# Two PSUM banks for the convolutions, ordered transfers in the even mixer, splits ahead of a norm and a shorter end in a two-layer decoder trunk

## The chip, the cores and the metric

The kernel runs on one core of a Trainium2 chip. The metric is the device time of one execution in microseconds (us), from which span, waits and clock are told apart by a profile of one such execution. Engines are called as in the profile: PE is TensorE (its matrix products), PEld its weight loads, DVE is VectorE, ACT ScalarE, POOL GpSimd; SP is a queue that only issues transfers. PE's clock has two levels, 1.2 and 2.4 GHz; a granted clock of 1.00 is the upper one, 0.50 the lower.

## What is computed

A trunk of two layers for 256 prompt tokens and 8 sample tokens of the same weights, model width 1024, inner width 2816 of each feed-forward network (FFN):

```python
def run_trunk(x, ...):
    for layer in range(DEPTH):                    # DEPTH = 2
        x = x + 0.5 * swiglu(rmsnorm(x, norm_g[layer, 0]), ff_in[layer, 0], ff_out[layer, 0])
        hn = rmsnorm(x, norm_g[layer, 1])
        # layer 0: even_mixer, layer 1: odd_mixer
        x = x + mix
        x = x + 0.5 * swiglu(rmsnorm(x, norm_g[layer, 2]), ff_in[layer, 1], ff_out[layer, 1])
    return rmsnorm(x, norm_f)

def even_mixer(h, s0, ...):      # gated linear attention beside a chunked spatial gate
    q, k, v, r, z, u_sg, v_sg = jnp.split(h @ w_in, EVEN_SPLITS, axis=-1)
    o, s_new = gla_recurrence(q, k, v, log_a, s0)
    out_a = rmsnorm(o, gla_g) * jax.nn.silu(r)
    out_b = gelu(u_sg) * (w_s @ layernorm(gelu(v_sg)) + sg_b)
    return jnp.concatenate([out_a, out_b], axis=-1) @ w_out, s_new, ...

def odd_mixer(h, conv_buf, pool_buf, ...):   # causal depthwise convolution beside causal pooling
    a, gt, xp = jnp.split(h @ w_in, ODD_SPLITS, axis=-1)
    out_c = jax.nn.silu(layernorm(depthwise_conv31(a * sigmoid(gt)) + conv_b))
    out_d = (mean of the last 2, 4, 8, 16 rows of xp, less xp) @ pool_w * pool_scale
    return jnp.concatenate([out_c, out_d], axis=-1) @ w_out, ...
```

The states of attention (gla), gate (sgv), convolution and pooling are outputs too.

## The kernel before, in words

Activations lie transposed, channels on the 128 partitions and T = 264 columns (256 prompt, 8 sample) in the free dimension. Every projection is a row of products 128 x 128 by 128 x 264. The weights are streamed: SP's queue loads chunks `raw` of 512 KB, ACT rounds each 128 x 1024 half of one to `hi`, DVE forms the rest `lo = raw - hi` (the "splits"), and PE makes three products for each block: activation's high part by `hi`, its low part by `hi`, its high part by `lo`. Tiles named `..h` and `..l` (`xh`, `xl`, `oyh`, `oyl`, `oah`, `oal`) are such high and low parts of activations.

The program is one instruction stream for each engine, written by Python code that runs generators (one for each task, such as `conv(i)`, `pooled(i)`, `sample_state(p)`) against a `Clock`: a planner that assigns each instruction a cost and a due time, and emits a split (`split_ahead`) when the engine is thought to be free. A task waits by `need` for what others `produce`, and by `acquire` for a buffer; `slot()` waits for a place between products. On the chip each engine runs its stream in this order, whatever is ready. Transfers that do not pass `keep_in_program_order` may be placed elsewhere in their queue by the scheduler behind the program.

Stages, in order: start, `ff00` (FFN of layer 0, first), even mixer (projections `evin_c`, output `ev_o`), `ff01`, `ff10`, odd mixer (`odin_c`, output `od_o`), `ff11` (the last FFN), end. A norm is a sum of squares (`odn_acc`, split in `ff_nh`, `ff_nl`, summed over partitions by PE to `ff_ss`) and a reciprocal root on DVE (`ff_v` to `ff_rb`) of nine steps; the projection runs before the norm is known, and `rb` is multiplied in when a column leaves PSUM. While `cur["chain"]` is set, between the last `od_o` column and the end of that root, `split_ahead` holds back lo splits that are more than one half chunk ahead of use.

In an FFN, column pairs a and g leave PSUM as `ff_ta = a * rb`, `ff_sa = silu(ff_ta)` (ACT) and `ff_g = g * ff_sa`; `g`'s `rb` is applied at the residual, `ff11n_r = ff_o * rb * 0.5`, `x += ff11n_r`.

In the even mixer the sample states S (2 of 512 KB) are loaded on POOL's queue, then `vb`, copies of the sample values spread over partitions (4 of 256 KB); ACT copies the layer-normed gate rows as `gv`, `vln`, which PE transposes (`trvln`).

In the odd mixer, ACT writes 32 copies `rr` of the gated values (8 for each of four channel groups), POOL's queue shifts each into place by a transfer, and `conv(i)` is 128 quarter products into a PSUM tile of the one `s2` buffer of 1024 columns, which ACT empties into `cv_i`. Their mean `mu` is a product again; DVE subtracts it. The pools are sums of shifted rows on DVE (`pw`, `pd`), one product `pp` each, which ACT and DVE split to `oyh`, `oyl`.

At the end ACT squares the last residual, PE sums (`fin_ss`), DVE takes a root of three columns (`rsqrt`, `fin_yi` and on), PE spreads it (`fin_pb`) and DVE multiplies; products `warm` of no use keep PE going in between.

## Time and profile before

| | |
|---|---|
| runs | 990.77, 988.93, 988.32 us; median 988.93 us |
| profiled execution | 990.54 us, of it the span of the trace 988.8 us |
| mean granted clock | 0.993 |
| busy share | PE 98%, PEld 96%, DVE 68%, ACT 50%, POOL 5% |
| chain that ended last | PE 91%, DVE 4%, ACT 2%, DMA 1%, issue 1% |
| transfers | 176.22 MB, mean 178 GB/s |

A busy PE means that a product is under way, not that it runs at full rate, since products overlap and the clock can be halved. So two views matter beside busy time: what each engine waited for, and the granted clock by stretches. In a timeline a row begins with start and length in us, and the bracket at its end is the engine's idle time ahead of it and what ended that. In a row of stretches come the length and then, for PE, PEld, DVE, ACT and POOL in turn, busy us and number of instructions.

### The profile page before, as it was taken

How to read it: one execution, taken by the hardware profiler on the slowest of the kernel's cores; microseconds unless marked ns; L12 is line 12 of the kernel's file. 1: busy time of each engine (PE TensorE's matmuls, PEld its weight loads, DVE VectorE, ACT ScalarE, POOL GpSimd, SP SyncE). 2: the span in 40 equal slices, each digit the busy share in tenths (PEclk: the TensorE clock that was granted, in tenths of full speed). 3: DMA queues.
4: the chain of work that ended last, by engine and by line, in shares of the span. 5: the costliest groups of instructions: out<-in, count | busy, mean ns of one | idle time of the engine just before them, and what ended most of it. 6: DMA issues, size and time to landing. Idle time of an engine off the chain costs nothing.

```text
span 988.8 us, 20086 instructions
## 1 busy us (share of the span) xinstructions
PE 970.9 (98%) x8258; PEld 953.7 (96%) x8258; DVE 671.3 (68%) x1072; ACT 493.1 (50%) x749; POOL 45.4 (5%) x105
## 2 busy tenths in 40 slices
PE   8999999999999999999999999999989999999997
PEld 7999999999899999999999999999978999999996
DVE  7866656678898876665667666566756886666552
ACT  6644444456376454444445444444474744444440
POOL 2000000030100000000000000000070000000000
PEclk9999999999999999999999999999999999999999
DMA  8755555562646575555555555555452566555531
GB/s 280 232 197 189 175 186 177 176 219 91 163 146 221 187 220 188 177 189 183 181 170 194 190 175 189 182 180 187 158 163 87 171 223 202 176 188 182 181 107 44
DMA packets 50555, 176.22 MB, mean 178 GB/s; under 512 B 6352, under 2 KB 6816, under 8 KB 50464
## 3 DMA queue, kind: packets, MB, share of 16 engines
q1 hardware_dynamic: 46800, 165.85, 51.0%
q0 software_dynamic: 3376, 8.68, 3.2%
q8 instruction: 65, 1.06, 0.5%
q10 hardware_dynamic: 288, 0.41, 0.1%
q14 instruction: 26, 0.21, 0.1%
HBM read 170.33 MB, written 3.42 MB: 176 GB/s over the span
## 4 chain that ended last, share of the span: by engine, by line
PE 91%; DVE 4%; ACT 2%; DMA 1%; issue 1%; SPq 0%; DVEq 0%; ACTq 0%
PE ff_c L316 50%; PE ff_o L316 26%; PE evin_c L316 5%; PE ev_o L316 2%; PE od_o L316 2%; PE odin_c L316 2%; DMA raw<-in_wts 1%; ACT rr L339 1%; PE conv L324 1%; DVE lo L339 1%; DVE start_xl L339 0%; DVE pd L339 0%; PE fin_ss L316 0%; PE o L316 0%; PE os L316 0%
## 5 line engine op out<-in xcount | busy, mean ns | idle before, releaser
L339 ACT ACTIVATE hi<-raw 128x1024 fp32r<-128x1024 f32 (+1 forms) x315 | 330.1, 1050 | 379.6 <-PE ff_c L316 207.9
L339 DVE TENSOR_TENSOR lo<-raw,hi 128x1024 fp32r<-128x1024 f32 (+1 forms) x315 | 382.0, 1216 | 162.0 <-ACT hi L339 160.9
L316 PE MATMUL ff_o<-ff_gh,hi 128*128 128x264 f32 x704 | 198.9, 283 | 0.0
L316 PE MATMUL ff_o<-ff_gl,hi 128*128 128x264 f32 x704 | 198.8, 282 | 0.0
L316 PE MATMUL ff_o<-ff_gh,lo 128*128 128x264 f32 x704 | 198.8, 282 | 0.0
L316 PEld LDWEIGHTS ff_o<-ff_gh,hi 128*128 128x128 f32 x704 | 132.1, 188 | 0.0
L316 PEld LDWEIGHTS ff_o<-ff_gh,lo 128*128 128x128 f32 x704 | 132.2, 188 | 0.0
L316 PEld LDWEIGHTS ff_o<-ff_gl,hi 128*128 128x128 f32 x704 | 132.2, 188 | 0.0
L316 PE MATMUL ff_c<-odn_xh,lo 128*128 128x264 f32 x352 | 99.8, 284 | 1.8 <-DVE lo L339 1.8
L316 PE MATMUL ff_c<-start_xh,lo 128*128 128x264 f32 x352 | 100.2, 285 | 1.1 <-DVE lo L339 1.1
L316 PE MATMUL ff_c<-start_xh,hi 128*128 128x264 f32 x352 | 99.9, 284 | 0.8 <-ACT hi L339 0.8
L316 PE MATMUL ff_c<-start_xl,hi 128*128 128x264 f32 x352 | 100.1, 284 | 0.0
L316 PE MATMUL ff_c<-odn_xh,hi 128*128 128x264 f32 x352 | 99.7, 283 | 0.0
L316 PE MATMUL ff_c<-odn_xl,hi 128*128 128x264 f32 x352 | 99.7, 283 | 0.0
L316 PE MATMUL ff_c<-ff01n_xh,lo 128*128 128x264 f32 x352 | 99.4, 283 | 0.0
L316 PE MATMUL ff_c<-ff01n_xh,hi 128*128 128x264 f32 x352 | 99.4, 282 | 0.0
L316 PE MATMUL ff_c<-ff01n_xl,hi 128*128 128x264 f32 x352 | 99.4, 282 | 0.0
L316 PE MATMUL ff_c<-evn_xl,hi 128*128 128x264 f32 x352 | 99.4, 282 | 0.0
L316 PE MATMUL ff_c<-evn_xh,hi 128*128 128x264 f32 x352 | 99.4, 282 | 0.0
L316 PE MATMUL ff_c<-evn_xh,lo 128*128 128x264 f32 x352 | 99.4, 282 | 0.0
L339 DVE TENSOR_TENSOR ff_g<-ff_c,ff_sa 128x264 f32<-128x264 f32 x88 | 37.7, 431 | 55.5 <-PE ff_c L316 55.5
L316 PEld LDWEIGHTS ff_c<-odn_xh,lo 128*128 128x128 f32 x352 | 66.6, 189 | 2.0 <-DVE lo L339 2.0
(366 smaller groups left out, 1927.7 us busy)
## 6 DMA issues: line engine op xcount, KB each, us to landing
raw<-in_wts SPq DMA_DIRECT2D x308, 512.0 KB, 3.4
raw<-in_wts SPq DMA_DIRECT2D x8, 256.0 KB, 5.1
rr<-gp POOLq DMA_DIRECT2D x32, 35.5 KB, 3.6
x<-in_xt SPq DMA_DIRECT2D x4, 264.0 KB, 4.7
S<-in_sgla POOLq DMA_DIRECT2D x2, 512.0 KB, 6.9
vb<-vbd POOLq DMA_DIRECT2D x4, 256.0 KB, 10.5
out_gla_s<-S POOLq DMA_DIRECT2D x2, 512.0 KB, 4.8
mat<-in_mats POOLq DMA_DIRECT2D x1, 640.0 KB, 5.2
```

Of the source, the lines that this page charges most:

```text
L316: return pe_run(nc.tensor.matmul(out, lhsT=lhsT, rhs=rhs, start=start, stop=stop), out, lhsT, rhs, cost)
L324: Clock.credit -= pe_run(nc.tensor.matmul(out, lhsT=lhsT, rhs=rhs, start=start, stop=stop), out, lhsT, rhs, cost)
L339: ins = tc.keep_in_program_order(f(*args, **kw))
```

## The change

Eight edits: the four convolutions share one PSUM tile and take its two banks (512 columns) in turn, and the planner's credit is not left negative behind them; the pools' products no longer wait for a slot; the root of three columns has seven steps in place of nine; in the last FFN `rb` is multiplied into the silu tile, so that the residual is one operation; the limit `chain` is gone; in the even mixer S is loaded in four pieces and the transfers of S, `vb`, `gla_s` and of `wz` are kept in program order; the planner takes 6.5 us in place of 4.2 for a chunk's landing there; a pad of 128 bytes per partition is put among the constants. The loop of the prompt's final state makes the same eight products in another order (not shown).

```diff
--- before.py
+++ after.py
@@ -227,6 +227,7 @@
     allones = cst.tile([P, P], F32R, name="allones")
     nc.vector.memset(allones.bitcast(F32), 1.0)
     warm = cst.tile([P, 256], F32, name="warm")
+    cst.tile([P, 32], F32, name="cst_pad")
     nc.vector.memset(warm, 0.0)
     nc.scalar.activation(cst.tile([P, 1], F32, name="first"), ones, AF.Silu)
     vec = cst.tile([P, NV], F32, name="vec")
@@ -255,7 +256,7 @@
              "msk": [0.0], "pr": [0.0] * 2}
     for t in ("ta", "sa", "gg", "rt", "sq", "oo", "osq", "pds", "pd"):
         locks[t] = [0.0] * 2
-    cur = {"slots": False, "chain": False, "rate": 300.0, "table": AF.Silu}
+    cur = {"slots": False, "land": 4200.0, "rate": 300.0, "table": AF.Silu}
 
 
     DELAY = {("dve", "dve"): 127.0, ("act", "act"): 143.0, ("dve", "act"): 128.0, ("act", "dve"): 142.0,
@@ -465,7 +466,6 @@
     xh, xl = [None] * KT, [None] * KT
     raw, raw_at, his, los, hi_at = {}, {}, {}, {}, {}
     state = {"chunk": 0, "hi": 0, "lo": 0, "idx": 0}
-    CHAIN = 1
     LEAD, MUST = 5, 8
 
     def load_chunk(issue=True):
@@ -475,7 +475,7 @@
         r = raw[c] = wraw.tile([P, CT * P], F32, tag="raw", name=f"raw{c}")
         if issue:
             tc.keep_in_program_order(nc.sync.dma_start(r[:, :n * P], a["wts"][c, :, :n * P]))
-            raw_at[c] = max([Clock.now] + [u[4] for u in uses.get(r.tensor.name, ())]) + 4200.0
+            raw_at[c] = max([Clock.now] + [u[4] for u in uses.get(r.tensor.name, ())]) + cur["land"]
             arrive(r, raw_at[c])
 
     def split_hi(q=0, parts=1):
@@ -552,8 +552,6 @@
         if (state["hi"] <= min(c + LEAD, state["lo"] + 2, NHALF - 1)) and E["act"] <= Clock.now + 200.0 \
                 and raw_at[state["hi"]] <= Clock.now + 200.0:
             split_hi()
-        if cur["chain"] and state["lo"] > c + CHAIN:
-            return
         if state["lo"] < state["hi"] and E["dve"] <= Clock.now + 200.0 and hi_at[state["lo"]] <= Clock.now + 200.0:
             split_lo()
 
@@ -592,14 +590,14 @@
         yi = sml.tile([P, n], I32, tag=f"yi{n}", name=f"{name}_yi")
         V.tensor_scalar(yi, v.bitcast(I32), -0.5, float(0x5F3759DF), op0=ALU.mult, op1=ALU.add)
         y = yi.bitcast(F32)
-        for it in range(3):
-            t = sml.tile([P, n], F32, tag=f"rt{n}", name=f"{name}_t{it}")
-            u = sml.tile([P, n], F32, tag=f"ru{n}", name=f"{name}_u{it}")
-            y2 = sml.tile([P, n], F32, tag=f"ry{n}", name=f"{name}_y{it}")
-            V.tensor_mul(t, y, y)
-            V.scalar_tensor_tensor(out=u, in0=t, scalar=-0.5, in1=v, op0=ALU.mult, op1=ALU.mult)
-            V.scalar_tensor_tensor(out=y2, in0=u, scalar=1.5, in1=y, op0=ALU.add, op1=ALU.mult)
-            y = y2
+        t = sml.tile([P, n], F32, tag=f"rt{n}", name=f"{name}_t")
+        V.tensor_mul(t, y, y)
+        V.tensor_mul(t, t, v)
+        V.scalar_tensor_tensor(out=t, in0=t, scalar=-10.0 / 3.0, in1=t, op0=ALU.add, op1=ALU.mult)
+        V.scalar_tensor_tensor(out=y, in0=t, scalar=5.0, in1=y, op0=ALU.add, op1=ALU.mult)
+        V.tensor_mul(t, y, y)
+        V.scalar_tensor_tensor(out=t, in0=t, scalar=-0.0263671875, in1=v, op0=ALU.mult, op1=ALU.mult)
+        V.scalar_tensor_tensor(out=y, in0=t, scalar=0.5625, in1=y, op0=ALU.add, op1=ALU.mult)
         return y
 
     def rsqrt_all(y, v, t):
@@ -696,7 +694,6 @@
         release("rt")
         release("rt")
         produce(f"{name}_rb", t)
-        cur["chain"] = False
 
     def columns(cols, evac, tag, src, lead=0, wide=False):
 
@@ -725,9 +722,7 @@
                     waiting.clear()
                     run_gens()
 
-    def resid(m, ps, rb, gcol, name, lock="mm"):
-        if m == KT - 1 and name == "odn":
-            cur["chain"] = True
+    def resid(m, ps, rb, gcol, name, lock="mm", half=False):
         t = 0.0
         if rb is not None:
             yield from acquire("rt")
@@ -736,6 +731,9 @@
                                                                 op0=ALU.mult, op1=ALU.mult),
                           lambda: V.tensor_add(x[m], x[m], s))
             release("rt")
+        elif half:
+            yield from do("dve", lambda: V.scalar_tensor_tensor(out=x[m], in0=ps[:, :T], scalar=0.5, in1=x[m],
+                                                                op0=ALU.mult, op1=ALU.add))
         else:
             yield from do("dve", lambda: V.tensor_add(x[m], x[m], ps[:, :T]))
         release(lock)
@@ -778,6 +776,8 @@
                     sil[j] = tmp.tile([P, T], F32, tag="sa", name=f"{name}_sa{j}")
                     w = yield from do("act", lambda: A.activation(sil[j], t, AF.Silu), after=w)
                     release("ta")
+                    if after is not None:
+                        w = yield from do("dve", lambda: V.tensor_mul(sil[j], sil[j], cur["rb"]), after=w)
                     produce(f"{name}_s{j}", w)
                 else:
                     yield from need(f"{name}_s{j}")
@@ -798,7 +798,7 @@
                 for k in range(JT):
                     wmm(ps[:, :T], (("ff_out", l, i), k, m * P, P), lambda: (gh[k], gl[k]), f"{name}_g{k}",
                         k == 0, k == JT - 1)
-                spawn_first(resid(m, ps, rb, next_g, f"{name}n"))
+                spawn_first(resid(m, ps, rb if after is None else None, next_g, f"{name}n", half=True))
                 if after is not None:
                     spawn(after(m))
                 run_gens()
...
+            def load(dst, src):
+                tc.keep_in_program_order(nc.gpsimd.dma_start(dst, src))
+
             def sample_load(p):
-                yield from need("vtok2", "xk11")
+                yield from need("vtok2", "xk11", *(["S0b"] if p else []))
                 yield from acquire("big")
                 S[p] = evb.tile([P, NB, P], F32, tag="big", name=f"S{p}")
-                nc.gpsimd.dma_start(S[p], a["sgla"][:, p])
-                arrive(S[p], Clock.now + 5000.0)
-                produce(f"S{p}", Clock.now + 5000.0)
+                for b in (0, 4):
+                    load(S[p][:, b:b + 4], a["sgla"][:, p, b:b + 4])
+                    yield 2500.0
+                produce(f"S{p}b")
+                arrive(S[p], Clock.now + 2500.0)
+                produce(f"S{p}", Clock.now + 2500.0)
 
             def sample_state(p):
                 yield from need(f"S{p}", "os")
                 yield from acquire("big")
                 vb = evb.tile([P, NB, P], F32, tag="big", name=f"vb{p}")
                 src = vbd.rearrange("b (p h d) -> p h b d", p=2, h=2)
+                if p:
+                    yield from need("vb0")
                 for h2 in range(2):
-                    nc.gpsimd.dma_start(vb[h2 * 64:(h2 + 1) * 64], src[p, h2].partition_broadcast(64))
-                arrive(vb, Clock.now + 6000.0)
-                yield 6000.0
+                    load(vb[h2 * 64:(h2 + 1) * 64], src[p, h2].partition_broadcast(64))
+                    yield 2500.0
+                produce(f"vb{p}")
+                arrive(vb, Clock.now + 3000.0)
+                yield 3000.0
                 t = [0.0] * NB
                 for b0 in (0, 4):
                     for b in range(b0, b0 + 4):
@@ -1109,7 +1121,7 @@
                         op0=ALU.mult, op1=ALU.add), after=t[b])
                 release("big")
                 release("big", E["dve"] + 4000.0)
-                nc.gpsimd.dma_start(o["gla_s"][:, p], S[p])
+                load(o["gla_s"][:, p], S[p])
 
             def sample_q():
                 yield from need("sa", "q0", "q1", "k0", "k1")
@@ -1350,9 +1362,11 @@
             spawn(sample_state(0), sample_state(1))
 
             spawn_first(z_col())
+            cur["land"] = 6500.0
             columns(even_in_cols(), evac, "evin", src)
             finish(*[f"ev_y{i}" for i in OUT_KS["ev_out"][0]])
             mixer_out("ev_out", yh, yl, next_g, "ev")
+            cur["land"] = 4200.0
 
 
     def odd_mixer(src, next_g, dg):
@@ -1415,19 +1429,24 @@
 
             def conv(i):
 
-                yield from need(f"shift{i}", "glu_in")
-                yield from acquire("s2")
-                ps = ps2.tile([P, 1024], F32, tag="s2", name=f"conv{i}")
+                yield from need(f"shift{i}", "glu_in", *([f"conv{i - 1}"] if i else []), *([f"cd{i - 2}"] if i > 1 else []))
+                if i == 0:
+                    yield from acquire("s2")
+                    keep["conv"] = ps2.tile([P, 1024], F32, tag="s2", name="conv")
+                ps = keep["conv"][:, 512 * (i % 2):512 * (i % 2) + 512]
                 for q in range(QUADS):
                     for j in range(4):
                         quarter(ps[32 * j:32 * j + 32, 0:SEQ], dg[i][:, q, j], shifted[i][:, j, 4 * q:4 * q + SEQ],
                                 q == 0, q == QUADS - 1, j)
                     yield 0.0
+                Clock.credit = max(Clock.credit, 0.0)
                 release("rr")
+                produce(f"conv{i}")
                 acc = cv[i][:, 0:SEQ]
                 t = yield from do("act", lambda: A.activation(acc, ps[:, 0:SEQ], AF.Identity,
                                                               bias=vec[:, V_CB + i:V_CB + i + 1]), after=Clock.now)
-                release("s2", t)
+                if i == 3:
+                    release("s2", t)
                 produce(f"cd{i}", t)
 
             def conv_sample(i):
@@ -1469,7 +1488,6 @@
             def pool_mm(i):
                 yield from need(f"pd{i}")
                 yield from acquire("s1")
-                yield from slot()
                 pp = s1_psum(f"pp{i}")
                 matmul(pp[:, :T], pw[:, i, :], pds[i])
                 release("pd")
@@ -1582,7 +1600,7 @@
 
     def gate_weights():
         yield 40000.0
-        nc.gpsimd.dma_start(wz, a["wz"])
+        tc.keep_in_program_order(nc.gpsimd.dma_start(wz, a["wz"]))
         arrive(wz, Clock.now + 4000.0)
         yield 8000.0
         yield from do("dve", lambda: V.tensor_mul(wz, wz, vec[:, V_NG + 8:V_NG + 16].unsqueeze(2).to_broadcast([P, KT, 32])))
```

How this moves instructions is seen in the order in which the engines run them. On ACT the four `cv`, which had a split between each two of them, stand in a row.

DVE behind the convolutions, before (`lo` are splits): `cvsum` adds up the convolutions, `cv<-cv,mu` subtracts their mean, `xp`, `xs`, `pw`, `pd` are a pool's steps.

```order
L339 TENSOR_REDUCE pss_9522<-xs 128x8
L339 SCALAR_TENSOR_TENSOR pd_9515<-pss_9522,xs 128x8
L339 TENSOR_TENSOR cvsum<-cv_8924,cv_8925 128x264
L339 TENSOR_TENSOR cvsum<-cvsum,cv_8926 128x264
L339 TENSOR_TENSOR lo_9577<-raw_9267,hi_9535 128x1024
L339 TENSOR_TENSOR cv_8924<-cv_8924,mu 128x264
L339 TENSOR_TENSOR cv_8925<-cv_8925,mu 128x264
L339 TENSOR_TENSOR cv_8926<-cv_8926,mu 128x264
L339 TENSOR_TENSOR cv_8927<-cv_8927,mu 128x264
L339 TENSOR_TENSOR xp_8905<-odin_c_9527,odin_rb 128x256
```

And now:

```order
L340 TENSOR_TENSOR cvsum<-cvsum,cv_8919 128x264
L340 TENSOR_TENSOR cv_8917<-cv_8917,mu 128x264
L340 TENSOR_TENSOR cv_8918<-cv_8918,mu 128x264
L340 TENSOR_TENSOR cv_8919<-cv_8919,mu 128x264
L340 TENSOR_TENSOR cv_8920<-cv_8920,mu 128x264
L340 TENSOR_TENSOR lo_9546<-raw_9142,hi_9516 128x1024
L340 TENSOR_TENSOR xp_8899<-odin_c_9332,odin_rb 128x256
L340 TENSOR_TENSOR xs<-odin_c_9332,odin_rb 128x8
L340 TENSOR_TENSOR pw_1_9567<-xp_8899 128x270
L340 TENSOR_TENSOR pw_2_9576<-pw_1_9567 128x268
L340 TENSOR_TENSOR pw_4_9583<-pw_2_9576 128x264
L340 TENSOR_TENSOR lo_9592<-raw_9163,hi_9559 128x1024
```

The lo splits and pool 2, which before stood ahead of the subtraction, now stand behind it; pool 1, pool 0 and one more split follow ahead of `oyl`.

POOL's queue in the even mixer, before (`out_` are outputs):

```order
L1088 DMA S_3219<-in_sgla 128x1024
L1081 DMA out_gla_p<-fs_sb 128x256
L1088 DMA S_3221<-in_sgla 128x1024
L1098 DMA vb_3523<-vbd 64x8x128 x2
L1098 DMA vb_3526<-vbd 64x8x128 x2
L1266 DMA out_sgv_p<-vln_2610 128x512
L1267 DMA out_sgv_s<-vln_2611 8x512
L1112 DMA out_gla_s<-S_3219 128x1024
L1112 DMA out_gla_s<-S_3221 128x1024
```

And now:

```order
L1083 DMA out_gla_p<-fs_sb 128x256
L1087 DMA S_3220<-in_sgla 128x512 x2
L1087 DMA S_3324<-in_sgla 128x512 x2
L1278 DMA out_sgv_p<-vln_2611 128x512
L1279 DMA out_sgv_s<-vln_2612 8x512
L1087 DMA vb_3570<-vbd 64x8x128 x2
L1087 DMA vb_3572<-vbd 64x8x128 x2
L1087 DMA out_gla_s<-S_3220 128x1024
L1087 DMA out_gla_s<-S_3324 128x1024
```

`out_gla_p` comes first, S in pieces, and the four `vb` loads behind the two `sgv` outputs.

DVE at the root ahead of the last FFN, before, from its last steps on:

```order
L339 TENSOR_TENSOR ff_s<-ff_rb 128x264
L339 SCALAR_TENSOR_TENSOR ff_s<-ff_s,ff_v 128x264
L339 SCALAR_TENSOR_TENSOR ff_rb<-ff_s,ff_rb 128x264
L339 TENSOR_TENSOR lo_10180<-raw_9903,hi_9999 128x1024
L339 TENSOR_TENSOR lo_10210<-raw_9966,hi_10100 128x1024
L339 TENSOR_TENSOR ff_ta_10178<-ff_c_10089,ff_rb 128x264
L339 TENSOR_TENSOR ff_ta_10208<-ff_c_10179,ff_rb 128x264
```

And now, the rows ahead of the root and its first step:

```order
L340 TENSOR_TENSOR x<-x,od_o_9974 128x264
L340 TENSOR_TENSOR lo_10092<-raw_9841,hi_9931 128x1024
L340 SCALAR_TENSOR_TENSOR odn_xl_10100<-x,vec,odn_xh_10099 128x264
L340 TENSOR_TENSOR odn_acc<-odn_acc,odn_sq_10106 128x264
L340 TENSOR_TENSOR lo_10119<-raw_9883,hi_9979 128x1024
L340 TENSOR_TENSOR ff_nl<-odn_acc,ff_nh 128x264
L340 TENSOR_TENSOR lo_10144<-raw_9946,hi_10080 128x1024
L340 TENSOR_SCALAR ff_v<-ff_ss 128x264
```

The two splits that followed `ff_rb` stand ahead of `ff_v`; behind `ff_rb` two evictions `ff_ta` follow at once.

## Rows read from the trace of the kernel before

**Rows 1.** The page, part 1: busy us, share of span, instructions.

```profile
PE 970.9 (98%) x8258; PEld 953.7 (96%) x8258; DVE 671.3 (68%) x1072; ACT 493.1 (50%) x749; POOL 45.4 (5%) x105
```

**Rows 2.** Waits of PE: line, releaser: us in total, times, longest.

```profile
PE ff_c L316 <- DVE lo L339: 2.9, 4, 1.8
...
PE conv L324 <- ACT cv L339: 2.6, 1, 2.6
...
PE trvln L327 <- ACT vln L339: 1.9, 1, 1.9
...
PE od_o L316 <- DVE oyl L339: 1.1, 1, 1.1
...
PE ev_o L316 <- DVE oal L339: 0.5, 1, 0.5
```

**Rows 3.** Stretches: busy us by engine, PEclk, DMA share, GB/s.

```profile
302.00:304.00 2.00, 2.00 (x10) 2.00 (x11) 1.87 (x4) 1.29 (x3) 0.00 (x1) 0.56 0.68 223
304.00:306.00 2.00, 2.00 (x12) 2.00 (x12) 2.00 (x4) 1.06 (x1) 0.54 (x1) 0.59 0.42 112
...
732.00:734.00 2.00, 0.22 (x2) 0.22 (x5) 0.00 (x0) 1.95 (x5) 2.00 (x5) 1.00 0.33 81
...
760.00:762.00 2.00, 2.00 (x9) 1.80 (x9) 1.38 (x7) 1.09 (x2) 0.00 (x0) 0.50 0.00 0
...
794.00:796.00 2.00, 2.00 (x11) 2.00 (x10) 2.00 (x4) 0.76 (x2) 0.00 (x0) 0.50 0.60 227
...
850.00:880.00 30.00, 30.00 (x252) 30.00 (x252) 19.04 (x27) 14.91 (x22) 0.00 (x0) 1.00 0.57 184
```

**Rows 4.** Timeline of DVE: the norm ahead of the last FFN.

```profile
788.33 0.43 DVE L339 TENSOR_SCALAR ff_v<-ff_ss 128x264 f32<-128x264 f32 x1 [1.61 <-PE ff_ss L316]
...
792.29 2.35 DVE L339 TENSOR_TENSOR lo<-raw,hi 128x1024 fp32r<-128x1024 f32 x2
```

**Rows 5.** Timeline of ACT in the even mixer.

```profile
255.52 0.42 ACT L339 ACTIVATE gv<-gv 128x264 f32<-128x264 f32 x1
...
257.79 1.06 ACT L339 ACTIVATE hi<-raw 128x1024 fp32r<-128x1024 f32 x1 [1.85 <-DMA raw<-in_wts]
```

**Rows 6.** DMA issues in 244 to 266: KB each, median us to landing.

```profile
raw<-in_wts SPq DMA_DIRECT2D x3, 512.0 KB, 8.2
...
vb<-vbd POOLq DMA_DIRECT2D x4, 256.0 KB, 10.5
```

**Rows 7.** The page, part 6: the same of the whole span.

```profile
raw<-in_wts SPq DMA_DIRECT2D x308, 512.0 KB, 3.4
...
rr<-gp POOLq DMA_DIRECT2D x32, 35.5 KB, 3.6
```

**Rows 8.** Timeline of ACT and PE around the convolutions.

```profile
733.26 0.47 ACT L339 ACTIVATE cv<-conv,vec 128x256 f32<-128x256 f32 x1
...
733.78 3.97 PE L324 MATMUL conv<-rr,dg 128*32 128x256 f32 x64 [2.56 <-ACT cv L339]
...
738.97 3.66 PE L324 MATMUL conv<-rr,dg 128*32 128x256 f32 x64
```

**Rows 9.** Timeline of POOL: issues of the shifted copies.

```profile
730.46 6.84 POOL L1397 DMA_DIRECT2D rr<-gp  x14 [0.99 <-DMA rr<-gp]
```

**Rows 10.** Timeline of DVE behind the convolutions.

```profile
749.71 1.45 DVE L339 TENSOR_TENSOR cv<-cv,mu 128x264 f32<-128x264 f32 x4 [4.33 <-PE mu L316]
...
757.43 0.48 DVE L339 SCALAR_TENSOR_TENSOR oyl<-pp,vec,oyh 128x264 fp32r<-128x264 f32 x1
```

**Rows 11.** Stretches again: VectorE's work on pool 2.

```profile
740.39:743.15 2.76, 2.76 (x49) 1.66 (x42) 2.59 (x10) 0.45 (x2) 0.71 (x2) 1.00 0.75 190
```

**Rows 12.** Timeline of PE and DVE at the end.

```profile
977.10 1.46 PE L316 MATMUL fin_ss<-warm 128*128 128x256 f32 x6
...
977.77 0.43 DVE L339 TENSOR_TENSOR x<-x,ff11n_r 128x264 f32<-128x264 f32 x1
...
980.19 0.16 DVE L339 SCALAR_TENSOR_TENSOR fin_u<-fin_t,fin_v 128x3 f32<-128x3 f32 x1
```

9 lines of the change are left out of this document (5 added, 4 removed).

## The prediction

> **What bounds the kernel now.** I read the page first, then what TensorE (PE) waits for, then its granted clock by stretches, and last the timeline around each wait. PE is busy 98% of the span [rows 1], so there is little to gain anywhere but in the few places where PE stands still or runs at half its clock. The view of waits names them: 1.9 us in the even mixer, where a transpose waits for ScalarE's copy `vln`; 2.6 us in the odd mixer, where the second convolution waits for ScalarE to empty the only PSUM tile; 1.1 us at the output product `od_o`, which waits for VectorE's `oyl`; a largest wait of 1.8 us of `ff_c` for a lo split; and 0.5 us at `ev_o` [rows 2]. The clock stands behind three of them: in the stretches after the wait at `ev_o`, after `od_o` and after `ff_c` the granted clock is 0.56, 0.50 and 0.50, that is, mostly or wholly the lower of its two levels (1.2 and 2.4 GHz), but around the longer wait for the convolution it is 1.00 [rows 3]. From 302 to 306 two windows of 2 us at 0.56 and 0.59 lose 0.88 + 0.82 = 1.7 us of a busy PE's work; I take that for each stretch. The sum below starts from the profiled execution, 990.54 us (span 988.8 us). The median of the runs shown is 988.93 us, 1.6 us less, about one such stretch; so I take it that the number of stretches differs from run to run.
>
> **The norm ahead of the last FFN (chain limit removed): -1.8 us, and the clock.** Before, no lo split was emitted between the last `od_o` column and `ff_rb`. VectorE idles 1.61 us ahead of `ff_v` at 788.33, runs the nine steps, and only then, at 792.29, makes two splits in 2.35 us; PE's wait of 1.8 us is for the first of these [rows 2, 4]. In the new order both splits that followed `ff_rb` stand earlier: one between a residual and `odn_xl`, one between `ff_nl` and `ff_v`. The second costs half of the 2.35, some 1.2 us, and fits into the 1.61 us of idle time. The first goes into a gap of about 0.6 us and delays the chain to `ff_nl` by about 0.5 us; most of VectorE's 1.61 us is PE still at other products ahead of `ff_ss`, so that this is hidden; if it were not, it costs 0.5. The next split then follows only two evictions, some 2 us ahead of its use. So 1.8 us go. With the wait gone nothing is left that preceded the half clock from 794 on, and 1.7 more go where the profiled run had it. The Trainium skill ("TensorE: Matmul & The Clock Gate", Part 1) says the clock's state depends on recent activity against a count that runs freely, so that one kernel shows different cold stretches from run to run; [rows 3], with a fall after a short wait and none after a longer one, agree. By that rule the 1.7 is no certain gain. I keep it, with 0 as the other end.
>
> **Even mixer (transfers kept in order, four loads): -1.5 us.** ScalarE has finished `gv` at 255.94 but a hi split stands next in its queue, ahead of `vln`, and waits 1.85 us for its raw chunk [rows 5]. That chunk takes long: the three raw transfers issued here have a median of 8.2 us to landing, the four 256 KB `vb` loads 10.5 [rows 6], against 3.4 for all 308 raw transfers [rows 7]. In the new order POOL's queue holds `gla_p` first, then four S pieces, and the `vb` loads only after the `sgv` outputs, about 15 to 20 us later. So 1 MB of `vb` no longer competes with the raw chunk, and I let it land before ScalarE is free: -1.85. Ends: 0, if S alone delays it as much; -2.0 at most, since PE reaches the transpose just before. On the other side three `ev_o` products now stand ahead of the pair of `ob`, whose result passes `oo`, a lo split and `oal` on VectorE before `ev_o` goes on; a product takes 0.12 us (252 in 30 us, [rows 3]), so the chain starts 3 x 0.12 us later and PE's wait grows by that: +0.36. The half clock behind it I leave as it is. The S halves themselves are needed late and cost nothing there.
>
> Against this edit stands the Trainium skill's page "DMA: Bandwidth & Descriptors" (Bandwidth, measured): batch transfers, since small ones reach less of the peak. Its fit has about 2 us of fixed time per transfer, so as an estimate four pieces one after the other would take about 4 us more than two halves; [rows 6], where 256 KB pieces take longer than the 512 KB raw chunks, cannot tell this from contention. By that rule the term of 1.85 would shrink towards 0 and the time be 1.85 us higher.
>
> **Odd mixer (one PSUM tile with two banks): +0.6 us.** The wait of 2.56 us is for `cv` of convolution 0, which stands behind 32 copies `rr` on ScalarE and starts at 733.26 [rows 8]. With two banks convolution 1 need not wait for it. What limits it now is the shifted copies: the last 14 are issued from 730.46 on, over 6.84 us [rows 9], and land 3.6 us later in the median [rows 7]. The 27 `odin_c` products that filled in between the convolutions come later (9 of them take 738.97 - 733.78 - 3.97 = 1.22 us, [rows 8]). So `mu`, and with it VectorE's `cv - mu` at 749.71 [rows 10], could come 2.56 + 3 x 1.22 = 6.2 us earlier, at 743.5, but for the last copies: issued by 736.8, landing about 740.4, so that convolution 3 ends near 744 and not at 741.3. I take a new wait of 2.0 us (ends 0.8 and 2.5): VectorE starts at 745.5.
>
> Then VectorE has more to do before `oyl`, for which PE waits. From 749.71 to 757.43 are 7.72 us [rows 10], with one lo split in it. In the new order three splits and all pools stand there: two splits more, 2.35, and pool 2, 2.76 us between 740.39 and 743.15 [rows 11]. Together 12.8 us: `oyl` starts at 758.3, against 757.43. The time that PE gains at the convolutions it loses at `od_o`: its wait grows from 1.1 (and the eviction's length) to about 3 us. That is +0.9 (ends -0.3 and +1.4). The dropping of the slot wait ("at once") lets PE reach the pool products early, where it waits for VectorE anyhow: 0. The shorter root saves two short steps there, but one split now stands ahead of the next `oyl`, 1.2 us; most of that lies under PE's 21 products and the slow clock, so net -0.4 to +0.8, of which I take -0.3, and +0.6 in all. The half clock behind this wait stays.
>
> **The last FFN: 0.** 22 products `sa` by `rb`, 0.43 us each as its sisters, come to 9.5 us on VectorE. In 850 to 880 it is busy 19.04 of 30 us, with PE at 30 of 30 [rows 3]; 2.2 us more in 30 fit. Uncovered they cost 9.5. Before the residual one operation of 0.43 per column goes.
>
> **The end: -0.5 us.** Of the last residual one of two operations of 0.43 goes, but the warm products end at 978.56 [rows 12], so that the next product starts only 0.2 to 0.4 earlier. The root loses two of nine steps of 0.16 us, nearly 0.4 us with the gaps between them, partly behind four more warm products. Ends -0.2 and -0.86.
>
> **The rest: -0.1.** The 128 KB of `wz` leave the first, crowded transfers; of PE's other waits for lo splits (2.9 - 1.8 = 1.1 us, [rows 2]) some may go: 0 to -0.6. The pad of 128 bytes shifts addresses: 0. The longer assumed landing moves hi splits a little later, where PE hasn't been waiting: 0.
>
> **Sum.** -1.8 - 1.7 - 1.85 + 0.36 + 0.6 - 0.5 - 0.1 = -5.0, so 985.5 in a run like the profiled one. In a run like the median, which had one stretch fewer, part of the 1.7 was not there to gain, but one of the two that I leave may fail too; I predict **985.3 us**.
>
> **The rivals.**
> *The gain is half eaten.* If the last shifted copies land at the late end, the split ahead of `oyl` is uncovered, and the raw chunk gains half only: 985.3 + 0.5 + 0.7 + 0.9 = 987.4; if the clock's 1.7 stays as well, 989.1. For it: VectorE has 12.8 us in one row, with no idle time. Against: its splits cannot get longer. 32%.
> *The stretches at half clock go as well* at `ev_o` or `od_o`: 985.3 - 1.7 = 983.6, both 981.9. Against: the wait at `od_o` grows. 13%.
> *The convolution does not do what it says*, since convolution 2 and 3 wait on the copies as much as before on `cv`: then VectorE's pile comes 2.6 us later still, 987.9. The issue rows, done by 737.3, speak against. 4%, counted with the first.
> *Slower: the new product on the last FFN is not covered.* It stands between silu and `ff_g`, so each of 22 PSUM pairs comes free 0.43 us later; if PE runs out of banks each time, 985.3 + 9.5 = 994.8; it decides from 6.6 of these 9.5 us on. The 11 us idle in 30 speak against. 4%.
> *Slower: the `vb` loads land on the raw chunks issued 268 to 273.* Three hi splits now stand in one row on ScalarE ahead of the S products. With 8.2 us instead of 3.4 each [rows 6, 7], up to 4.8 us of delay, and 1.7 for the clock: 991.8, with any more of it slower than no change. 3%.
>
> **Chances.** The forecast, 983.9 to 986.6, has 48%. About 0.3%, 3.0 us, is what a measurement of this kernel tells from no change: faster is below 985.96, slower above 991.9. Of the forecast 40 points lie below 985.96, with the 13 for the clock 53; slower 7, the rest 40. The range leaves out the cases of both lost clocks and the slower ones: 982.3 to 989.1.
>
> **What would show it.** No wait of PE for `vln` over 0.5 us, and raw chunks at 250 landing in under 6 us; convolution 1 starts by 732; PE's wait for `oyl` near 3 us; no wait for a lo split near 790, and a clock of 1.00 after it; FFN stretches with PE at 30 of 30. Wrong would be the forecast if VectorE's row at the pools shrinks or grows by over 2 us, if a wait for hi splits appears at 280 to 290, or if a slow stretch stands at 790.

## The result and the profile after

The changed kernel takes **997.08 us** (median of 4 runs, 995.98 to 998.22), against 988.62 us (4 runs) of the kernel before on the same chip: ratio 1.0084, 95% interval 1.006 to 1.0107. It is 8.5 us slower; the forecast of 985.3 us and its range are missed on the upper side. The profiled execution took 998.22 us, its span is 996.4 us, 7.6 us longer than that of before.

The page after, part 1, for [rows 1]: busy time, share of the span and instructions.

```profile
PE 976.5 (98%) x8258; PEld 961.9 (97%) x8258; DVE 674.0 (68%) x1080; ACT 493.4 (50%) x749; POOL 46.9 (5%) x107
```

PE runs the same 8258 products and is busy 5.6 us longer with them. So most of the loss is no wait at all: either the clock was lower in places, or the same products took longer. The waits of PE (in total, times, longest), for [rows 2]:

```profile
PE conv L325 <- ACT cv L340: 5.0, 3, 3.8
PE od_o L317 <- DVE oyl L340: 1.7, 1, 1.7
...
PE ff_c L317 <- DVE lo L340: 1.1, 3, 0.5
PE od_o L317 <- DVE xs L340: 1.1, 1, 1.1
PE ev_o L317 <- DVE lo L340: 0.9, 1, 0.9
PE ev_o L317 <- DVE x L340: 0.5, 1, 0.5
PE ob L317 <- DVE oo L340: 0.5, 1, 0.5
PE ev_o L317 <- DVE oal L340: 0.5, 1, 0.5
...
PE trvln L328 <- ACT vln L340: 0.2, 1, 0.2
```

Two waits are gone, that for `vln` (1.9, now 0.2) and the long one of `ff_c` for a lo split (1.8, now at most 0.5). But the convolutions, which were to wait no more, wait three times for `cv`, 5.0 us instead of 2.6, and `ev_o` has two waits that it didn't have. The timeline after (start, length; in the bracket the idle time ahead and what ended it) at these places, for [rows 5, 8, 10, 12]:

```profile
256.51 1.06 ACT L340 ACTIVATE hi<-raw 128x1024 fp32r<-128x1024 f32 x1 [0.21 <-DMA raw<-in_wts]
...
279.84 1.06 ACT L340 ACTIVATE hi<-raw 128x1024 fp32r<-128x1024 f32 x1 [2.91 <-DMA raw<-in_wts]
282.56 1.06 ACT L340 ACTIVATE hi<-raw 128x1024 fp32r<-128x1024 f32 x1 [1.67 <-DMA raw<-in_wts]
...
286.58 0.78 DVE L340 TENSOR_TENSOR obl<-mxt,obh 128x264 fp32r<-128x264 f32 x2 [3.22 <-ACT obh L340]
...
730.56 3.66 PE L325 MATMUL conv<-rr,dg 128*32 128x256 f32 x64
...
737.52 0.47 ACT L340 ACTIVATE cv<-conv,vec 128x256 f32<-128x256 f32 x1
...
738.05 5.66 PE L325 MATMUL conv<-rr,dg 128*32 128x256 f32 x64 [3.83 <-ACT cv L340]
744.27 3.97 PE L325 MATMUL conv<-rr,dg 128*32 128x256 f32 x64 [0.56 <-ACT cv L340]
748.80 3.97 PE L325 MATMUL conv<-rr,dg 128*32 128x256 f32 x64 [0.56 <-ACT cv L340]
...
754.98 1.45 DVE L340 TENSOR_TENSOR cv<-cv,mu 128x264 f32<-128x264 f32 x4 [5.77 <-PE mu L317]
...
767.58 0.48 DVE L340 SCALAR_TENSOR_TENSOR oyl<-pp,vec,oyh 128x264 fp32r<-128x264 f32 x1
...
985.75 0.43 DVE L340 SCALAR_TENSOR_TENSOR x<-ff_o,x 128x264 f32<-128x264 f32 x1 [6.11 <-PE ff_o L317]
...
989.62 0.92 PE L317 MATMUL fin_pb<-con,fin_yi 128*128 128x128 f32 x6
```

Convolution 1 begins 0.06 us after `cv` of convolution 0 is done, though it writes the other bank. The hi split at 256.51 is on time, those at 279.84 and 282.56 aren't. Stretches after, for [rows 3] (length, then busy us and instructions of PE, PEld, DVE, ACT, POOL; granted clock; DMA share; GB/s):

```profile
302.00:304.00 2.00, 1.67 (x7) 1.67 (x8) 1.79 (x5) 0.91 (x3) 0.00 (x0) 0.58 0.94 305
...
740.00:742.00 2.00, 2.00 (x24) 1.99 (x20) 0.00 (x0) 0.00 (x0) 2.00 (x5) 0.50 0.20 46
...
770.00:772.00 2.00, 2.00 (x10) 1.80 (x9) 1.86 (x7) 1.12 (x2) 0.00 (x0) 0.50 0.00 0
...
798.00:802.00 4.00, 4.00 (x35) 4.00 (x34) 3.32 (x7) 1.89 (x2) 0.00 (x0) 1.00 0.81 245
804.00:808.00 4.00, 4.00 (x35) 4.00 (x35) 3.85 (x7) 2.09 (x4) 0.00 (x0) 1.00 0.21 61
...
150.00:180.00 30.00, 30.00 (x246) 30.00 (x245) 18.04 (x25) 13.35 (x19) 0.00 (x0) 1.00 0.56 181
...
460.00:490.00 30.00, 30.00 (x253) 30.00 (x252) 18.68 (x25) 13.84 (x19) 0.00 (x0) 1.00 0.58 189
...
645.00:675.00 30.00, 30.00 (x246) 30.00 (x245) 18.61 (x26) 13.67 (x18) 0.00 (x0) 1.00 0.54 181
...
856.00:886.00 30.00, 30.00 (x250) 30.00 (x249) 20.90 (x31) 13.78 (x21) 0.00 (x0) 1.00 0.54 185
```

The clock is 1.00 beside and behind the root ahead of the last FFN (798 to 802, 804 to 808), but 0.50 inside convolution 1, which takes 5.66 us instead of the 3.97 of [rows 8]. And in two output stages, at 150 and 645, there are 246 products in 30 us at full clock and with PE never idle, where there are 253 at 460. The kernel before has 253 at 645 too:

```profile
645.00:675.00 30.00, 30.00 (x253) 30.00 (x252) 18.31 (x24) 13.84 (x19) 0.00 (x0) 1.00 0.57 190
```

Nobody waits there, and the view of waits is silent about it. Last, the transfers (KB each, median us to landing): first those issued at 244 to 266, for [rows 6], then those at 266 to 284.

```profile
raw<-in_wts SPq DMA_DIRECT2D x3, 512.0 KB, 5.8
...
raw<-in_wts SPq DMA_DIRECT2D x4, 512.0 KB, 10.0
vb<-vbd POOLq DMA_DIRECT2D x4, 256.0 KB, 8.6
```

In the kernel before the latter had no `vb` beside them:

```profile
raw<-in_wts SPq DMA_DIRECT2D x4, 512.0 KB, 5.5
```

### The profile page after: what moved, and what is told of

It reads as the page before. It is cut to its first block, busy times and chain, and to the rows that moved or that the text cites. A ratio compares the mean times of both kernels' runs of the same rounds, so it can differ in the third digit from the quotient of the medians.

```text
span 996.4 us, 20087 instructions
## 1 busy us (share of the span) xinstructions
PE 976.5 (98%) x8258; PEld 961.9 (97%) x8258; DVE 674.0 (68%) x1080; ACT 493.4 (50%) x749; POOL 46.9 (5%) x107
## 4 chain that ended last, share of the span: by engine, by line
PE 88%; DVE 5%; DMA 2%; ACT 2%; issue 1%; SPq 0%; DVEq 0%; ACTq 0%
PE ff_c L317 50%; PE ff_o L317 26%; PE evin_c L317 3%; PE ev_o L317 2%; PE od_o L317 2%; DMA raw<-in_wts 2%; PE odin_c L317 2%; DVE lo L340 1%; PE conv L325 1%; ACT rr L340 1%; DMA x<-in_xt 1%; DVE vln L340 0%; PE fin_ss L317 0%; DVE pd L340 0%; ACT hi L340 0%
## 5 line engine op out<-in xcount | busy, mean ns | idle before, releaser
L317 PE MATMUL ff_o<-ff_gh,hi 128*128 128x264 f32 x704 | 201.4, 286 | 0.0
L317 PE MATMUL ff_o<-ff_gh,lo 128*128 128x264 f32 x704 | 201.3, 286 | 0.0
L317 PE MATMUL ff_o<-ff_gl,hi 128*128 128x264 f32 x704 | 201.3, 286 | 0.0
L340 DVE TENSOR_TENSOR ff_g<-ff_c,ff_sa 128x264 f32<-128x264 f32 x88 | 37.7, 431 | 45.5 <-PE ff_c L317 44.8
L317 PEld LDWEIGHTS ff_c<-start_xh,lo 128*128 128x128 f32 x352 | 65.9, 187 | 2.4 <-DVE lo L340 2.3
```

The source lines that it names most:

```text
L317: return pe_run(nc.tensor.matmul(out, lhsT=lhsT, rhs=rhs, start=start, stop=stop), out, lhsT, rhs, cost)
L340: ins = tc.keep_in_program_order(f(*args, **kw))
```

## The experiments

Each was timed beside the kernel before, whose median lay between 988.62 and 990.31 us. Ratios are to before, with 95% intervals.

**One part of the change alone, or all but one.** Six kernels: only the pad; all but the pad; only the test of `cur["chain"]` (two lines) removed from `split_ahead`; only the conv edit; only the even mixer's edits (with `wz` in order, the longer landing and the reordered products of the prompt's final state); and the change with the convolutions of before.

```diff
# before_pad (after_nopad is the change without this line)
+    cst.tile([P, 32], F32, name="cst_pad")
# before_nochain
-        if cur["chain"] and state["lo"] > c + CHAIN:
-            return
# before_conv: the hunk of conv(i) alone; after_oldconv: all but it
+                ps = keep["conv"][:, 512 * (i % 2):512 * (i % 2) + 512]
# before_even: the hunks of sample_load, sample_state, final state, land and wz alone
+                    load(S[p][:, b:b + 4], a["sgla"][:, p, b:b + 4])
```

> The kernel before with nothing but the pad of 128 bytes among its constants, which moves every SBUF tile behind it. In the changed kernel the time from product to product, constant within a stage, is not what it was: 123.3 ns in place of 121.3 in the output products of the first FFN and 123.3 in place of 120.0 in those of the third, 121.3 in place of 120.0 in the input products of the second and the last FFN, 120.0 in place of 121.3 in those of the first; about 4 us more in all. Theory A, the pad does it (addresses): the same pattern appears here, and about 4 us more than before, 992 to 993 us. Theory B, the distance settles by chance at the start of each stage in each execution: another pattern, and 986 to 991 us. Theory C, the order of the other engines' work does it: the pattern of the kernel before (121.3 in the first FFN, 120.0 elsewhere), 988.6 us.

> The changed kernel without the pad. Theory A (addresses): the products' distances are those of the kernel before, 121.3 ns in the first FFN and 120.0 elsewhere, and about 4 us go: 993 us. Theory B (chance): another pattern, 993 to 998 us. Theory C (order of work): the pattern of the changed kernel stays, 997 us.

> The kernel before without the limit on lo splits at the last norm, nothing else changed. The forecast's term: the wait of 1.8 us of the last FFN's input products goes, and the stretch at half clock behind it: 985.1 to 986.8 us, with no wait for a lo split near 790 us. Rival: the first of the moved splits delays the norm, so that the wait moves to the sum of squares or the first evictions: 988.6 us.

> The kernel before with the two-bank convolutions alone. In the changed kernel's trace each convolution still waits for the eviction of the one ahead, though that lies in the other bank, and VectorE's work piles up behind the mean. Theory 1: that is this edit's own doing: waits of 3.8, 0.6 and 0.6 us at the convolutions and about 2 us more at the output products, 5 to 7 us more in all: 993.6 to 995.6 us. Rival: the shift of other work in the changed kernel (splits, transfers) made it: within 1.5 us of 988.6.

> The kernel before with the even mixer's edits alone (S in four loads, transfers in program order, the longer assumed landing, the prompt state's loop, wz in order). In the changed kernel's trace the wait for vln is gone (1.9 us), but the output products wait 0.9 us for a lo split, 0.5 for oo and 0.5 for x besides the 0.5 for oal. Theory 1: the edit by itself gains nothing, up to 0.8 us slower, and the products' distances are as in other runs (120 ns, 121.3 in a stage or two): 988.5 to 990 us. Theory 2: it also brings the larger distances (121.3 in the second FFN's input, 123.3 in an output stage) that both profiles of the changed kernel show: 991 to 993.5 us. The forecast's term: 1.5 us faster, 987.4.

> The changed kernel with the convolutions as before, one PSUM tile each. The edit alone on the kernel before cost 6.1 us (995.0 against 989.0). Theory 1: it costs the same here, 991 us, and what is above the kernel before comes from elsewhere. Rival: the parts do not add, because the convolution's waits also cover others: 987 or less, or 994 and more.

| kernel | median us | ratio, interval |
|---|---|---|
| before_pad | 989.21 | 1.001 [0.9984, 1.0035] |
| after_nopad | 995.9 | 1.0061 [1.0039, 1.0084] |
| before_nochain | 985.58 | 0.9971 [0.9949, 0.9993] |
| before_conv | 995.04 | 1.0057 [1.0038, 1.0076] |
| before_even | 988.22 | 1.0005 [0.9986, 1.0024] |
| after_oldconv | 991.45 | 1.0029 [1.0016, 1.0041] |

The pad does nothing that can be measured. The chain limit's removal gains 3.4 us, the even mixer's edits nothing. The convolution's edit alone costs 6.1 us and has the same waits at `conv` and `od_o` as after (5.0, 1.7 and 1.1 us). Its profile accounts for the cost: 2.4 us more of waits at `conv`, 1.7 more at `od_o`, and convolution 1 (granted clock 0.50 from 731 to 735) takes 6.29 us instead of 3.97; that is 6.4 us in all. But without it the rest of the change is still slower than before, where chain limit and end should have gained 4 us: something else costs about as much as the convolution.

**Why the convolutions wait.** In the changed kernel the odd convolutions get a PSUM tile of their own in place of the second half of one tile. All engines run the same order.

```diff
-                    ps = keep["conv"][:, 512 * (i % 2):512 * (i % 2) + 512]
+                bank = "s1" if i % 2 else "s2"
+                yield from acquire(bank)
+                ps = s1_psum(f"conv{i}") if i % 2 else ps2.tile([P, 1024], F32, tag="s2", name=f"conv{i}")
```

> The changed kernel with the convolutions in two PSUM tiles, the odd ones in a buffer of the s1 pool, in place of two halves of one tile; every engine's order is the same. Theory 1: the wait for the eviction was due to the one tile; now convolution 1 starts when its copies have landed, 3 us or more earlier, 2 and 3 without the waits of 0.6 us, and the mean and the pools some 5 to 6 us earlier: 990.5 to 992 us. Rival: the copies' landings limit it, or PE only waits longer at the output products for VectorE's row: 995 us and more.

991.66 us, ratio 1.0034 [1.0016, 1.0051]. The waits for `cv` fall from 5.0 to 0.4 us, and the stage from the first `odin_c` to the first `od_o` takes 51.5 us (58.8 after). So the wait came with the tile, not with the bank: the program's semaphores make a product that writes any part of a tile wait for the engine that still reads another part of it. The Trainium skill ("PSUM — Partial Sum Buffer", PSUM bank collisions raise a hardware error) asks only for a guard by bank and quadrant; this program's guard was by tile. The runs with two tiles agree with that rule: in the profile of after_conv2t_al, further down, ScalarE empties convolution 1 until 733.09 while convolution 2 runs in the other bank from 732.77.

**What else costs 5 us.** The third part of the change (chain limit, shorter root, last FFN and residual) alone, on the kernel before:

> The kernel before without the limit on splits, with the product of rb in the last FFN, the residual in one operation and the root of seven steps; mixers as before. The limit alone gave 3.4 us. Theory 1: the product is hidden and the end gives 0.5 to 0.9 us more: 984.7 to 985.1 us, with the last FFN's input products at 30 of 30 us busy. Rival: the product delays the banks or brings the larger distance between products in the last FFN: 986.5 us and more.

990.97 us, ratio 1.0033 [1.0007, 1.0058]: slower, though the first of these edits alone gains 3.4 us. Its windows show the slow stages again, two of four output stages:

```profile
645.00:675.00 30.00, 30.00 (x246) 30.00 (x245) 17.32 (x23) 14.08 (x19) 0.00 (x0) 1.00 0.54 178
...
930.00:960.00 30.00, 30.00 (x246) 30.00 (x245) 15.14 (x18) 13.62 (x18) 0.00 (x0) 1.00 0.42 141
```

Each output stage has the same 528 products (704 x 3 over the four stages), and PE waits in none of them. From the first `ff_o` to the next stage are 63.36 us in the fast ones and 65.11 in the slow: 1.75 us each. From product to product this is 120.0 and 123.3 ns, the same through the whole stage. (A window's number also holds the products that are under way at its edges, some 2.5, so that 252 or 253 stand for 120.0 and 246 for 123.3.) What the edits share that could do this is where buffers lie: the shorter root needs two tile names less in the small pool `sml` (`ru` and `ry`, two buffers of [P, 3] each, 32 bytes apiece), and all that is placed behind it moves by 128 bytes against the weights ahead of it. Three kernels test it. `before_gap` is the kernel before with two unused tiles that shift by 128 bytes, every engine's order unchanged; the two others put two unused tiles back where `ru` and `ry` were.

```diff
# before_gap
+        for g in ("pa", "pb"):
+            sml.tile([P, n], F32, tag=f"{g}{n}", name=f"{name}_{g}")
# chain_end_al and after_al
+        for g in ("ru", "ry"):
+            sml.tile([P, n], F32, tag=f"{g}{n}", name=f"{name}_{g}")
```

> The kernel before with two unused tiles, 128 bytes per partition in all, ahead of the root's tiles, so that the activations of the FFN's output products (ff_gh, ff_gl) and of the odd mixer lie 128 bytes further from the weights (hi, lo); nothing else is changed, and every engine's order is the same. So far every kernel in which this distance is an odd multiple of 128 bytes (all with the shorter root) has output stages at 123.3 ns from product to product, and none in which it is a multiple of 256. Address theory: of the four FFN output stages some two or three run at 123.3 ns, 1.75 us each, and the time is 3 to 5 us longer: 992 to 994 us. Rival (the distance between products comes from the work on other engines, or from chance): no stage at 123.3, 988.9 us.

> The kernel of the run chain_end, 991.0 us, with two unused tiles in place of those that the shorter root no longer takes, which puts the activations back to a multiple of 256 bytes from the weights. Address theory: no output stage at 123.3 ns, and 4.5 to 6 us less: 985 to 986.5 us, with the end's gain of some 0.5 us to be seen in the trace alone. Rival (the product of rb in the last FFN is what costs): 991 us.

> The changed kernel with the same two unused tiles; its pad of 128 bytes lies ahead of weights and activations alike and moves both. Address theory: no stage at 123.3 ns, and 3.5 to 5 us less than 997.1: 992 to 993.5 us, what is left being the convolutions' 6 us less the chain's 3.4. Rival: 996 us and more.

before_gap: 992.68 us, 1.0049 [1.0012, 1.0085]. Its windows, one fast and one slow output stage:

```profile
150.00:180.00 30.00, 30.00 (x253) 30.00 (x252) 18.90 (x27) 13.65 (x18) 0.00 (x0) 1.00 0.55 184
...
645.00:675.00 30.00, 30.00 (x246) 30.00 (x245) 17.80 (x25) 13.36 (x18) 0.00 (x0) 1.00 0.53 179
```

chain_end_al: 985.42 us, 0.9958 [0.9921, 0.9995], against 990.97 without the two tiles. after_al: 991.96 us, 1.0015 [0.9986, 1.0045], against 997.08. The windows of after_al where after had 246:

```profile
150.00:180.00 30.00, 30.00 (x252) 30.00 (x252) 18.89 (x27) 13.82 (x19) 0.00 (x0) 1.00 0.52 178
...
645.00:675.00 30.00, 30.00 (x252) 30.00 (x251) 18.50 (x26) 13.04 (x18) 0.00 (x0) 1.00 0.54 181
```

So 128 bytes that no instruction uses cost 3 us, and two unused tiles give back 5 (by the medians; by the ratios to before it is 5 and 7, and neither is known to better than some 3 us). By the addresses of the compiled programs, the products' activations `ff_gh`, `ff_gl` lie 128 bytes off a multiple of 256 from the weights `hi`, `lo` in the six kernels without the right spacing (after, after_nopad, after_oldconv, after_conv2t, chain_end, before_gap): in their six profiles 13 of 24 FFN output stages run at 123.3 ns. In the twelve others, where the distance is a multiple of 256, none of 48 does. Two more sets of products bear this out. The activations of the FFNs' input products, `xh` and `xl`, lie at a multiple of 256 from the weights in all eighteen kernels, and none of their 72 input stages runs at 123.3 ns. Those of the odd mixer's output products, `oyh` and `oyl`, move with `ff_gh` and `ff_gl`; `od_o` runs at 123.3 in three of the six kernels (after, after_nopad, before_gap) and in none of the twelve. That the pair of operands is the cause, and not another pair that the same 128 bytes part, is only argued.

**Mended in both places:** convolutions in two tiles and the two unused tiles together.

> The changed kernel mended in two places: convolutions in two tiles (alone 991.7 us) and the activations at a multiple of 256 bytes from the weights. Address theory: no stage at 123.3 ns, 987 to 988 us, about the kernel before. Rival: 991 us.

984.65 us, ratio 0.9956 [0.9925, 0.9988]: faster than before, and 7.3 us faster than after_al, which differs in the convolution's tiles alone. PE and DVE here:

```profile
725.22 7.11 PE L325 MATMUL conv<-rr,dg 128*32 128x256 f32 x128
...
732.77 7.42 PE L325 MATMUL conv<-rr,dg 128*32 128x256 f32 x128 [0.44 <-ACT cv L340]
...
742.41 1.45 DVE L340 TENSOR_TENSOR cv<-cv,mu 128x264 f32<-128x264 f32 x4 [4.70 <-PE mu L317]
```

The four convolutions, 64 products each in the trace, run in two rows with one gap of 0.44 us; the shifted copies, for which the forecast set 2.0 us, hold nothing up. `cv - mu` starts 44.8 us behind the first `odin_c` (697.66), against 51.0 before. From that product to the first `ff_c` of the last FFN the odd mixer takes 82.6 us here, 83.8 before and 90.2 in after.

**Where the even mixer's gain goes.** In after, the `vb` loads are issued at 266 to 269 together with raw chunks, which take 10.0 us; ScalarE's hi splits at 279.84 and 282.56 wait 2.91 and 1.67 us for such chunks, the S products, a table load and `obh` stand behind them, VectorE waits 3.22 us for `obh`, and PE at `ev_o` for VectorE's lo. Four kernels on the mended one tell whether `vb` is the cause: without the even mixer's edits; with `vb` asked for 7 us later on the planner's clock; and with `vb` made to wait on the chip, by a small write of VectorE to its tile, at two places.

```diff
# mended_vblate
+                if p == 0:
+                    yield 7000.0
# mended_vb7
+                if p == 0:
+                    yield from do("dve", lambda: V.tensor_copy(vb[:, 0, 0:8], sa[:, 0:8]))
# mended_vb20
+                if p == 0:
+                    yield 4000.0
+                    yield from do("dve", lambda: V.tensor_copy(vb[:, 0, 0:8], sa[:, 0:8]))
```

mended_noeven takes back the hunks of before_even.

> The kernel mended in both places (convolutions in two tiles, alignment restored: 984.65 us, ratio to before 0.9956), with the first vb load of the even mixer asked for 7 us later on the planner's clock. Theory: the 3 us that the even mixer's edits gain at vln are given back because the vb loads land on the raw chunks issued at 268 to 273 (median 10.0 us to landing in 266 to 284, 5.5 before), so that a hi split of ScalarE waits 2.48 us at 281 ahead of the S products. With vb later, the raw chunks issued at 267 to 271 land in 4 to 5 us, that wait goes, and PE's wait of 1 to 1.8 us at ev_o goes with it: about 983.2 us, ratio 0.994. Rival: vb comes too late then, ScalarE and VectorE wait for it ahead of the S products, the wait at ev_o stays or grows: 984.7 us or more. Second rival: the raw chunks are slow for another reason (S outputs, or the queue of raw chunks itself); then they take 8 to 10 us here too and the time stays within 0.5 us of 984.65.

> The kernel mended in both places (984.65 us, ratio 0.9956) without the even mixer's edits (S in two loads, order left to the scheduler, wz not in order, shorter assumed landing). Theory: these edits are neutral, as in the kernel before (988.22 against 988.84 us): the wait for vln of 1.9 us comes back, and the waits for lo splits at ev_o shrink; 984.3 to 985.3 us, ratio 0.995 to 0.9965. Rival: in the mended kernel the edits cost 1 us by the late raw chunks: 983.6 or less. Rival: they gain the 1.5 us of the forecast: 986.1 or more.

> In mended_vblate the vb loads were issued at 266 to 269 as before, since a later place on the planner's clock changes only the order on ScalarE and VectorE, not the time of an issue on POOL. Here the first vb load really waits: VectorE writes one column of its tile first, behind the mixed gate rows mxt, at about 273 instead of 266. Theory (vb slows the raw chunks): the raw chunks issued at 267 to 270 land in about 5 us, those behind in up to 8, the third hi split of ScalarE no longer waits 2.5 us at 281, the wait of 1.8 us at ev_o goes to under 1: ratio to before 0.991 to 0.994. Rival (the raw chunks are slow on their own account): they still take about 10 us and the hi split still waits near 281, ratio 0.995 as without the wait. Cost of the added copy: under 0.2 us of VectorE.

> The same with VectorE's write 4 us later on the planner's clock, behind a row of work that ends near 286: the vb loads are issued some 20 us later than in the mended kernel, behind all raw chunks up to 281. Theory: raw chunks of 266 to 284 land in 4 to 6 us, as in the kernel without the even mixer's edits (5.3), ScalarE's hi split does not wait at 281, and the wait for a lo split at ev_o goes; ratio 0.990 to 0.993 unless vb, landing near 296, holds VectorE's S products ahead of oo (then ev_o waits 1 to 3 us for oal: 0.993 to 0.996). Rival (not vb): raw chunks at 10 us all the same.

mended_vblate: 982.27 us, 0.9916 [0.9885, 0.9947]. It did not do what it was for: POOL issues the loads at 266.10 as before, since the planner's clock moves nothing but order, and the raw chunks still take 10.5 us. mended_noeven: 983.68 us, 0.9925 [0.99, 0.9951]; its `vb` loads go out at 247 to 251, and raw chunks at 266 to 284 take

```profile
raw<-in_wts SPq DMA_DIRECT2D x4, 512.0 KB, 5.3
```

mended_vb7: 984.61 us, 0.9954 [0.9937, 0.9971]. The loads are issued at 273.21; the transfers at 266 to 284, and the hi split that waited:

```profile
raw<-in_wts SPq DMA_DIRECT2D x4, 512.0 KB, 4.9
vb<-vbd POOLq DMA_DIRECT2D x4, 256.0 KB, 5.9
```

```profile
277.27 1.06 ACT L340 ACTIVATE hi<-raw 128x1024 fp32r<-128x1024 f32 x1 [1.93 <-PE evin_c L317]
278.35 1.28 ACT L340 ACT_TABLE_LOAD   x1
```

Two of the three hi splits now stand in one row and the third waits for PE, not for a transfer; the table load comes 4.8 us earlier than in the mended kernel (283.15). The wait of `ev_o` for lo is gone (1.8 there), and the two stages of the mixer take 114.6 us in the profiles, against 116.7. The medians don't show these 2 us: 984.61 and 984.65. Nor is one profile each enough: in seven kernels without the even mixer's edits the same two stages take 113.4 to 116.3 us. mended_vb20: 992.25 us, 1.0038 [1.0023, 1.0054]. Here the loads are issued at 285.49. The raw chunks at 266 to 284 are fast (4.7 us), but those at 284 to 300 are hit. ScalarE's hi split at 295.84 waits 5.64 us for one, VectorE's lo split 5.47 us for that, and PE for what VectorE does behind it:

```profile
raw<-in_wts SPq DMA_DIRECT2D x6, 512.0 KB, 10.4
vb<-vbd POOLq DMA_DIRECT2D x4, 256.0 KB, 10.3
```

```profile
PE ob L317 <- DVE oo L340: 10.6, 1, 10.6
```

Where raw chunks are issued beside or behind the row of four loads, they take about twice as long (10.0, 10.5 and 10.4 us, against 4.7 to 5.5 without). In mended_vb7, whose last raw chunk of this stretch was issued 2.3 us ahead of the first load (270.87 against 273.21), they do not (4.9). The slow chunks move with `vb`; that is shown. The four mended kernels with ratios from 0.9916 to 0.9956 can't be ranked by these intervals; all of them beat both kernels.

## Why the prediction was wrong

| part | forecast, us | by the runs, us |
|---|---|---|
| chain limit, with its clock | -3.5 | -3.4 (before_nochain) |
| even mixer | -1.5 | about 0 (before_even -0.6, within its interval), see below |
| convolutions and pools | +0.6 | +6.1 (before_conv, without the pools' slot) |
| spacing of the operands | none | +5.1 (after against after_al) |
| last FFN | 0 | 0 by the trace |
| end | -0.5 | -0.8 by the trace |

The right column adds up to +7.0, the measured difference is +8.5; the intervals are wide enough for the rest (the spacing alone is +6.8 by the ratios).

**The step that failed in the odd mixer** is "With two banks convolution 1 need not wait for it". I took the buffer's two banks for two resources, and looked only for what would limit the convolution instead (the copies). The wait was not removed but lengthened, 2.56 to 3.83 us: `cv` still stands behind all `rr` copies and is done 7.4 us behind the start of convolution 0, before and after (733.73 - 726.28 and 737.99 - 730.56), but the 9 `odin_c` products that filled 1.2 us of this time are gone from there. Two more of 0.56 us appear where before the `odin_c` products covered the eviction, and after a PE idle for 3.83 us the clock fell to 0.50 inside convolution 1 (5.66 us instead of 3.97). That rival, "the convolution does not do what it says", had 4% and the wrong mechanism, the copies. What was built on the step held: VectorE's row from `cv - mu` to `oyl` was forecast at 12.8 us and takes 767.58 - 754.98 = 12.60; PE's wait at `od_o` near 3 us is 1.7 + 1.1 = 2.8. With two tiles `cv - mu` is 6.2 us earlier, and that is the forecast's own 6.2 without its copies.

**The step that failed for the FFNs** was hardly a step: "The pad of 128 bytes shifts addresses: 0", and of the shorter root only its time was counted. For the pad it is right (1.001), since it moves weights and activations together. But the tiles that the root no longer needs move them against each other by the same 128 bytes, and that costs about 5 us at a busy PE. No row of before could show it, for all its output stages ran at 120 to 121.3 ns; the forecast should have had a chance for it all the same, in a kernel whose PE is busy for 98% of the time and that can lose by a rate of 3%. Of the 5.1 us, 13 slow stages in 24 explain 4 x 13/24 x 1.75 = 3.8; what the rest is stays open.

**The even mixer:** the first half was right (the wait for `vln` 1.9 to 0.2 us, raw chunks 5.8 instead of 8.2), the sum not. The step that failed is that `vb`, moved 20 us later, costs nothing where it lands: the waits for hi splits at 280 to 290, which the forecast named as a sign against itself, are there. In the profiles the loss is even larger than the gain: from the first `evin_c` to the next `ff_c` the seven kernels with these edits and `vb` where the change put it take 116.0 to 117.4 us (mean 116.9), the seven without 113.4 to 116.3 (mean 115.2). An eighth without them, chain_end_al, is left out; its profile has a long stretch at half clock there. The rival at 3% names the place ("the `vb` loads land on the raw chunks issued 268 to 273"), but I priced it only as a disaster of 4.8 us and gave the case in which it merely returns the gain no chance. The Trainium skill's rule for large transfers ("DMA: Bandwidth & Descriptors", Measured) did not decide it: the raw chunk issued among the four S pieces landed in 7.5 us, less than the 9.2 of the one issued among the two halves before; neighbours in time set the landing, 4.7 to 10.5 us in the median for the same 512 KB.

**Right:** the chain limit, by place, and by size as far as the interval (0.7 to 5.0 us) tells: no wait of PE at the last norm, clock 1.00 behind it. How much of the 3.4 us is clock isn't shown: the 1.6 us between profile and median of the kernel before, which the forecast took for one stretch at half clock, may as well be the first FFN of that profile, whose products ran at 121.3 ns (1584 x 1.3 ns = 2.1 us). The last FFN's added product is covered: PE is busy 30.00 of 30 us with VectorE at 20.90, 1.9 more than in [rows 3]; the wait of PE that would show it isn't there, and chain_end_al, which has this product, runs no slower than before_nochain, which hasn't (985.42 and 985.58). The end: from the last residual's start (985.75) to `fin_pb` 3.87 us against 4.57, from the start of the last `ff_o` to the span's end 11.0 us against 11.8.
